# End of each FFN of a streaming encoder step: last down weights split in the scheduled list, the norm's shift taken off in PSUM, last output rows finished on VectorE

## The chip, the cores and the metric

One core of a Trainium2 chip runs the whole program in one launch. The metric is the device time of one execution in microseconds; of several runs the median is taken. Engine names in the profile: PE is TensorE's matmul, PEld its weight load, DVE is VectorE, ACT is ScalarE, POOL is GpSimd, SP is the engine that issues most DMAs.

## What is computed

Two layers of a streaming encoder on 512 prompt rows and 64 sample rows (576 in all) of width 1024, in fp32. Each layer is a mixer and then a gated FFN with a causal convolution of width 3; both are followed by a post-norm. Cut to what matters here:

```python
def layer_norm(x, g, b):
    mu = jnp.mean(x, axis=-1, keepdims=True)
    var = jnp.mean(jnp.square(x - mu), axis=-1, keepdims=True)
    return (x - mu) * lax.rsqrt(var + LN_EPS) * g + b

def conv_ffn(x, conv_state, w_up, conv_w, conv_b, w_down):
    hc, new_state = causal_dwconv(x @ w_up, conv_state, conv_w, conv_b)
    g, u = jnp.split(hc, 2, axis=-1)                 # 2 x 2816 columns
    return (jax.nn.gelu(g) * u) @ w_down, new_state

for layer in range(2):
    xp = layer_norm(ALPHA * xp + mixer(xp), ln_mix_g[layer], ln_mix_b[layer])     # same for xs
    f, new_conv = conv_ffn(xp, state, ffn_w_up[layer], ...)
    xp = layer_norm(ALPHA * xp + f, ln_ffn_g[layer], ln_ffn_b[layer])
```

## The kernel before

The state x lies transposed in SBUF: 8 tiles m of 128 features by 576 rows. Every product is made of three matmuls on numbers split in two: a high part rounded to the matmul's type and the rest as a low part (hh and hl of the hidden state, hi and lo of a weight). The rows go in two halves, so that one product fits a PSUM bank; the halves are 288 and 288 columns, in the last norm (n4) 320 and 256.

A weight comes by DMA into one of four `raw` buffers (SP). ScalarE copies it into the high part and VectorE subtracts that for the low part: a split (lines 307 and 308 outside the list below, 1277 and 1280 in it). `pump` (line 291) makes the next split of the weights in the order of the program, if its load has been issued and a slot is free; a freed buffer lets SP issue the next load.

The middle of an FFN is written as a list, `Plan`. Each operation names its engine, its cost, what it reads and what it writes; matmuls stay in the program's order and give due times, and each other engine takes the ready operation that is due first. An operation that no matmul in the list depends on has no due time and is taken when its engine has nothing else that is ready. The list holds the 22 blocks of the hidden width, each with its up weights, convolution, gelu and product, and the down products, which go through the list in chunks. The last chunk (blocks 17 to 21, 5 k-tiles) has 8 weights `dl[0]` to `dl[7]`, one for each tile m of x, 640 columns wide. The products of m = 0, 1, 2 stand at the end of the list (matmuls of line 1202, six banks, k outermost: 18 matmuls for each k). Block 21's hidden part is written last and is read by their last k. In the list the splits of m = 0 to 4 are made; the slots of m = 4 to 7 are those of the up weights of block 21.

After the list come, in program order on each engine: the posts of m = 0 and 1 (VectorE adds a bank to a tile of x, line 486, and sums tile 0 and tile 1 to `s1r`, line 489); two transposes that bring out the new conv state; then a `sweep` over m = 3 to 7 for the first half of the rows and a `sweep` for the second (matmuls of lines 417 to 419). A hook c of a sweep is called when c triplets of matmuls have gone; a weight has 5 triplets.

- `weights(5)`, `weights(6)`, `weights(7)` at hooks 1, 6 and 8 make the splits of m = 5, 6, 7.
- `shift` at hook 4: the norm takes off a common shift, which keeps its sums small. One matmul for each half turns `s1r` into the mean over the 256 features of tiles 0 and 1, on all partitions (`mone4` holds 4/1024, line 497); ScalarE copies it to `cs`; VectorE subtracts it from all 8 tiles, both halves: 16 instructions (line 507). Tiles 3 to 7 get their last product later, on top of it. Then m = 2 is posted.
- `acc` (lines 522 to 530) follows each tile: ScalarE squares it, the squares are summed to `a2` on VectorE (line 514), and the tiles to `a1`, on GpSimd for the early tiles and VectorE for the last. `a1` takes `s1r`'s buffers.
- Pumps at hooks 13, 17 and 21 (first FFN alone), for the first weights of the next layer.
- In the second sweep: `stats` of the first half (line 545, single-column matmuls on `a1` and `a2`, then small VectorE and GpSimd instructions, line 550 on), and the normalisation.

In the last FFN the second half of the output is different: `fin_early` at hooks 5, 9 and 13 transposes x's tiles 0 to 3 for the row blocks 0 to 2 (line 1758), since the output is by rows. The blocks 0 to 2 are finished within the second sweep (`fin_a`), blocks 3 and 4 at the end: `fin_q0` on VectorE for the left 512 columns (lines 1788, 1790), `fin_norm` on ScalarE for the right ones (line 1795), then `fin_q1`, a multiply and an add, block 4's on VectorE and block 3's on GpSimd (lines 1799, 1800). `fin_out` (line 1771) issues each output on SP, 256 KB.

Memory: the norm's pool `lnp` is opened at the left after the list, in the place of the list's sums of x; the FFN's pool is closed after the conv state's output.

## Time and profile before

| | us |
|---|---|
| median of 3 runs | 1305.2 (1304.25 to 1306.86) |
| profiled execution | 1306.91 |
| its span, first to last instruction | 1304.7 |
| PE busy in the span | 1243.1 |
| DVE busy | 1020.2 |
| ACT busy | 665.4 |
| POOL busy | 603.8 |

The span is what the trace covers; the rest of the execution lies around it. Busy time of an engine is an average over stages. The end of the first FFN lies at about 640 to 690 us, that of the last at about 1240 to 1305.

### The profile page before, as it was taken

Reading aid. Unit: us, or ns where it says so; the run is one execution under the profiler, and the core shown is the slowest. Engines: PE = TensorE matmul, PEld = TensorE weight load, DVE = VectorE, ACT = ScalarE, POOL = GpSimd, SP = SyncE. Lnnn points to the kernel's source line nnn. Section 1 sums busy time; section 2 is a strip of 40 time slices with the busy share of each in tenths; the row PEclk is TensorE's granted clock in tenths of the full one; section 3 lists DMA queues with packets and bytes.
Section 4 is the critical chain, followed back from the end, with each engine's and each line's share of the span. In section 5 each row is a group of like instructions: output and inputs, shape, how many; then the busy total and the mean of one; then the engine's idle time right before and its main releaser. Section 6 shows DMA issues by size and latency. Waiting matters only on the chain.

```text
span 1304.7 us, 23742 instructions
## 1 busy us (share of the span) xinstructions
PE 1243.1 (95%) x9087; PEld 1201.6 (92%) x9087; DVE 1020.2 (78%) x1895; ACT 665.4 (51%) x1064; POOL 603.8 (46%) x652
## 2 busy tenths in 40 slices
PE   8999999998999999999979998998999999999974
PEld 8999888998999999999979788998999999999974
DVE  4547786789998989887775339878999898878767
ACT  4553544457565556565343232347656566556432
POOL 3223222676465457364163015666654656545124
PEclk9999999999999999999979998999999999999987
DMA  8416320307675867666131422214657668866412
GB/s 224 127 33 183 99 82 14 100 12 169 147 168 128 191 150 177 153 159 145 56 97 49 145 65 73 68 35 101 155 140 180 141 147 192 170 150 147 93 36 73
DMA packets 204565, 155.76 MB, mean 119 GB/s; under 512 B 6524, under 2 KB 187036, under 8 KB 204452
## 3 DMA queue, kind: packets, MB, share of 16 engines
q1 hardware_dynamic: 192324, 111.96, 30.1%
q0 software_dynamic: 12128, 42.30, 18.3%
q8 instruction: 71, 1.16, 0.4%
q14 instruction: 42, 0.34, 0.1%
HBM read 107.07 MB, written 5.22 MB: 86 GB/s over the span
## 4 chain that ended last, share of the span: by engine, by line
PE 67%; DVE 14%; issue 9%; ACT 4%; POOL 3%; DMA 2%; ACTq 0%; SPq 0%; DVEq 0%; POOLq 0%
PE mm L1202 32%; PE aux L1202 16%; PE mm L417 4%; PE mm L418 4%; PE mm L419 4%; POOL x L585 2%; DVE x L507 1%; DVE raw L1355 1%; DVE wloA L308 1%; PE aux L545 1%; PE o L1094 1%; DMA wloB<-raw 1%; DVE x L486 1%; DVE pt L1045 1%; ACT pt L1041 1%
## 5 line engine op out<-in xcount | busy, mean ns | idle before, releaser
L1315 DVE SCALAR_TENSOR_TENSOR y<-hb,vecF,y 128x578 f32<-128x578 f32 x176 | 165.8, 970 | 6.3 <-ACT y L1305 4.9
L308 DVE TENSOR_TENSOR wloA<-raw,whiA 128x1024 fp32r<-128x1024 f32 (+2 forms) x54 | 65.3, 1225 | 98.4 <-ACT whiA L307 98.4
L1202 PE MATMUL mm<-xh,wloB 128*128 128x288 f32 x384 | 113.6, 296 | 0.0
L1202 PE MATMUL mm<-xh,whiB 128*128 128x288 f32 x384 | 113.5, 296 | 0.0
L1202 PE MATMUL mm<-xl,whiB 128*128 128x288 f32 x384 | 113.5, 296 | 0.0
L1254 POOL TENSOR_TENSOR raw<-raw 128x512 f32<-128x512 f32 x40 | 59.3, 1482 | 88.2 <-DVE wloB L1252 38.3
L1202 PE MATMUL mm<-xh,whiA 128*128 128x288 f32 x320 | 94.7, 296 | 5.4 <-ACT xh L1370 3.6
L417 PE MATMUL mm<-xh,whiA 128*128 128x288 f32 (+2 forms) x320 | 96.6, 302 | 3.2 <-ACT xh L641 3.2
L419 PE MATMUL mm<-xh,wloA 128*128 128x288 f32 (+2 forms) x320 | 95.2, 298 | 1.5 <-DVE wloA L308 1.5
L1202 PE MATMUL mm<-xl,whiA 128*128 128x288 f32 x320 | 95.2, 297 | 1.0 <-DVE xl L1372 1.0
L418 PE MATMUL mm<-xl,whiA 128*128 128x288 f32 (+2 forms) x320 | 95.3, 298 | 0.5 <-DVE xl L642 0.5
L1202 PE MATMUL mm<-xh,wloA 128*128 128x288 f32 x320 | 94.8, 296 | 0.0
L1329 POOL COPY stage<-hb 128x4 f32<-128x4 f32 x88 | 51.3, 680 | 90.8 <-DVE hb L1474 71.9
L1305 ACT ACTIVATE y<-hb,vecF 128x578 f32<-128x578 f32 x88 | 74.6, 865 | 32.1 <-DVE hb L1474 21.8
L307 ACT ACTIVATE whiA<-raw 128x1024 fp32r<-128x1024 f32 (+2 forms) x54 | 54.5, 1022 | 61.8 <-PE mm L817 44.4
L1438 DVE TENSOR_TENSOR x<-x,aux 128x288 f32<-128x288 f32 x160 | 71.2, 448 | 17.8 <-PE aux L1202 16.8
L1202 PE MATMUL aux<-hh,wloA 128*128 128x288 f32 x272 | 80.4, 295 | 1.5 <-DVE wloA L1413 1.5
L1202 PE MATMUL aux<-hh,whiA 128*128 128x288 f32 x272 | 80.5, 296 | 0.3
L1202 PE MATMUL aux<-hh,whiB 128*128 128x288 f32 x272 | 80.3, 295 | 0.0
L1202 PE MATMUL aux<-hh,wloB 128*128 128x288 f32 x272 | 80.2, 295 | 0.0
L1202 PE MATMUL aux<-hl,whiA 128*128 128x288 f32 x272 | 80.1, 294 | 0.0
L1202 PE MATMUL aux<-hl,whiB 128*128 128x288 f32 x272 | 80.0, 294 | 0.0
(432 smaller groups left out, 4712.0 us busy)
## 6 DMA issues: line engine op xcount, KB each, us to landing
raw<-in_ffn_w_up_dram SPq DMA_DIRECT2D x88, 512.0 KB
wloA<-raw POOLq DMA_DIRECT2D x40, 512.0 KB, 5.1
wloB<-raw POOLq DMA_DIRECT2D x40, 512.0 KB, 4.9
draw<-in_ffn_w_down_dram SPq DMA_DIRECT2D x80, 192.0 KB
raw<-in_w_in_o_dram SPq DMA_DIRECT2D x16, 512.0 KB
raw<-in_w_in_e_dram SPq DMA_DIRECT2D x14, 512.0 KB
raw<-in_ffn_w_down_dram SPq DMA_DIRECT2D x16, 320.0 KB
raw<-in_w_out_e_dram SPq DMA_DIRECT2D x8, 512.0 KB
```

What stands on the lines that cost most here:

```text
L307: ACT.activation(u.hi[:, c], u.raw[:, c], AF.Copy)
L308: DVE.tensor_sub(u.lo[:, c], u.raw[:, c], u.hi[:, c])
L417: PE.matmul(o, wh, h[:, k, a:b], start=first, stop=False)
L418: PE.matmul(o, wh, l[:, k, a:b], start=False, stop=False)
L419: PE.matmul(o, wl, h[:, k, a:b], start=False, stop=last)
L585: POOL.tensor_scalar(xk, xk, g, bb, op0=OP.mult, op1=OP.add)
L1202: PE.matmul(bank[key][:, :w], lhs(), rhs(), start=first, stop=stop)
L1254: plan.add("POOL", 1.3, lambda: POOL.tensor_add(R(2, b_), R(2, a_), R(2, b_)), r2, r2[1:], True, tag=f"s1_{j}")
L1305: plan.add("ACT", 0.86, lambda: ACT.activation(y, t[:, 2:580], AF.Identity, scale=V[:, 88 + ct:89 + ct], bias=V[:, 132 + ct:133 + ct]), hr ...
L1315: plan.add("DVE", 0.82, lambda q=q, y=y, t=t, ct=ct: DVE.scalar_tensor_tensor(y, t[:, q:q + 578], V[:, 44 * q + ct:44 * q + ct + 1], y, op ...
L1329: plan.add("POOL", 0.4, lambda s=s, t=t: POOL.tensor_copy(stage[:, :, s * NJ + j].rearrange("p (a b) -> p a b", a=2), t[:, 448:580].rearra ...
L1438: DVE.tensor_add(xm, xm, bank[key][:, :H2])
```

## The change

- `split_plain` is called for all 8 last down weights, so that m = 5, 6 and 7 are split in the list, too; the hooks `weights` are gone.
- In a norm that follows an FFN (`short`), `shift` subtracts from tiles 0 and 1 alone. For every other tile and half one more matmul, with `nmone4` = -4/1024, goes into the bank that holds the tile's last product (`unshift`, through `extra` in `sweep`), so that the post adds the shifted value. `a1` gets buffers of its own, since `s1r` is read until the last bank.
- `shift` stands at hook 2 instead of 4, the pumps of the first FFN at 5, 9 and 13 instead of 13, 17 and 21, `fin_early` at 12, 17 and 22 instead of 5, 9 and 13.
- The conv state's output goes ahead of the posts of m = 0 and 1, and the FFN's pool is closed before the norm's is opened.
- Blocks 3 and 4: the right 512 columns are read out of PSUM by VectorE with the mean taken off and the gain multiplied, and scaled with the bias added in a second instruction; ScalarE and GpSimd have no part in it, and each of the four outputs follows its own instruction.

```diff
--- before.py
+++ after.py
@@ -358,6 +358,8 @@
     DVE.memset(ones, 1.0)
     mone4 = consts.tile([128, 8], FR, name="mone4")
     DVE.tensor_scalar(mone4, mone, 4.0, None, op0=OP.mult)
+    nmone4 = consts.tile([128, 8], FR, name="nmone4")
+    DVE.tensor_scalar(nmone4, mone, -4.0, None, op0=OP.mult)
     nhalf = consts.tile([128, 8], FT, name="nhalf")
     DVE.memset(nhalf, -0.5)
     cmask = ev.tile([128, 128], FT, name="cmask")
@@ -418,7 +420,7 @@
         PE.matmul(o, wh, l[:, k, a:b], start=False, stop=False)
         PE.matmul(o, wl, h[:, k, a:b], start=False, stop=last)
 
-    def sweep(us, half, h, l, post, outer=False, hooks=None, ks=None):
+    def sweep(us, half, h, l, post, outer=False, hooks=None, ks=None, extra=None):
         hooks = dict(hooks or {})
         cnt = 0
         ks = ks or list(range(us[0].nk))
@@ -429,9 +431,11 @@
                 hooks.pop(c)()
             if banks[i] is None:
                 banks[i] = mmbank()
-            triplet(banks[i], us[i], k, h, l, half, k == ks[0], k == ks[-1])
+            triplet(banks[i], us[i], k, h, l, half, k == ks[0], k == ks[-1] and extra is None)
             cnt += 1
             if k == ks[-1]:
+                if extra is not None:
+                    extra(half, banks[i])
                 post(i, half, banks[i])
         for c in sorted(hooks):
             hooks[c]()
@@ -497,7 +501,7 @@
                 PE.matmul(bk[:, :b - a], mone4[:, 0:1].to_broadcast([128, 128]), self.s1r[half], start=True, stop=True)
                 self.cs[half] = self.tmp("cs", half)
                 ACT.activation(self.cs[half], bk[:, :b - a], AF.Copy)
-            for m in (2, 3, 0, 1, 4, 5, 6, 7):
+            for m in (0, 1) if self.short else (2, 3, 0, 1, 4, 5, 6, 7):
                 for half in range(2):
                     a, b = self.halves[half]
                     xm = x[:, m, a:b]
@@ -507,6 +511,11 @@
                         (DVE if m < 6 or self.short else POOL).tensor_sub(xm, xm, self.cs[half])
                     if m < 2:
                         self.acc(m, half)
+
+        def unshift(self, half, bk):
+
+            a, b = self.halves[half]
+            PE.matmul(bk[:, :b - a], nmone4[:, 0:1].to_broadcast([128, 128]), self.s1r[half], start=False, stop=True)
 
         def drain(self, half):
             if half in self.pend:
@@ -524,7 +533,7 @@
             sq = lnp["p"].tile([128, self.W], FT, name="sq", bufs=3)[:, :b - a]
             ACT.activation(sq, xm, AF.Square)
             if m == 1:
-                self.a1[half] = self.tmp("s1r", half)
+                self.a1[half] = self.tmp("a1" if self.short else "s1r", half)
                 POOL.tensor_add(self.a1[half], x[:, 0, a:b], xm)
             else:
                 (DVE if m >= self.dve else POOL).tensor_add(self.a1[half], self.a1[half], xm)
@@ -1552,7 +1561,7 @@
         for j in range(2, NJ):
             window(up[j], up.get(j + 1), j - 1, DOWNS[j])
         assert dn["run"] == len(dq)
-        for m in range(5):
+        for m in range(8):
             split_plain(dl[m], m // 4, m % 4)
         tail_of(NJ - 1)
         cut["h"] = norm.halves
@@ -1563,25 +1572,14 @@
                     s = dl[0].slots[k]
                     w = sl(0, m)
                     for n, (e, q) in enumerate(((0, 0), (0, 1), (1, 0))):
-                        mm(("K", m, half), kb[m, half], k == 0 and n == 0, k == dl[0].nk - 1 and n == 2,
+                        mm(("K", m, half), kb[m, half], k == 0 and n == 0, k == dl[0].nk - 1 and n == 2 and m < 2,
                            lambda m=m, e=e, k=k: (dl[m].hi, dl[m].lo)[e][:, 128 * k:128 * k + 128],
                            lambda q=q, s=s, a=a, b=b: (hh, hl)[q][:, s, a:b], (w[2 * e + k // 4], ("hidden", s, "hl"[q])), w=b - a,
                            took=0.0065 + (b - a) * 0.000439, tag=f"K{m}.{half}")
         plan.emit()
         st["dma"], st["freed"] = loaded["dma"], loaded["freed"]
         tes.close()
-        open_ln()
         banks = {k: bank["K", k[0], k[1]] for k in kb}
-        for i in range(2):
-            for half in range(2):
-                norm.post(i, half, banks[i, half])
-        live["A"] -= 3
-
-        def plain_split(u, w):
-            u.hi, u.lo = w
-            split_part(u, 0)
-            free_raw(1)
-
         bk = auxbank()
         sT = ytile()[:88, :256].rearrange("p (q c) -> p q c", q=2)
         for q in range(2):
@@ -1592,26 +1590,31 @@
             nc.sync.dma_start(dram(O[12 + q], layer * 4 * DFF, [[128, 88], [1, 128]]), sT[:, q])
         fes.close()
 
+        open_ln()
+        for i in range(2):
+            for half in range(2):
+                norm.post(i, half, banks[i, half])
+        live["A"] -= 3
+
         def shift():
             norm.shift()
             for half in range(2):
+                norm.unshift(half, banks[2, half])
                 norm.post(2, half, banks[2, half])
 
-        def weights(m):
-            return lambda: plain_split(dl[m], S[1][m - 4])
-
-        return dl[3:8], {1: weights(5), 4: shift, 6: weights(6), 8: weights(7)}
+        return dl[3:8], {2: shift}
 
     def ffn_tail(rest, norm):
         us, hooks = rest
-        hooks.update({c: pump for c in (13, 17, 21)})
+        hooks.update({c: pump for c in (5, 9, 13)})
         post = lambda i, hf, b: norm.post(3 + i, hf, b)
-        sweep(us, 0, hh, hl, post, hooks=hooks)
+        sweep(us, 0, hh, hl, post, hooks=hooks, extra=norm.unshift)
         hooks = norm.hooks(0, (7, 9, 11, 15))
-        sweep(us[0:1], 1, hh, hl, post)
+        sweep(us[0:1], 1, hh, hl, post, extra=norm.unshift)
         live["A"] -= 1
         pump(1)
-        sweep(us[1:], 1, hh, hl, lambda i, hf, b: post(i + 1, hf, b), hooks={c - 5: f for c, f in hooks.items()})
+        sweep(us[1:], 1, hh, hl, lambda i, hf, b: post(i + 1, hf, b), hooks={c - 5: f for c, f in hooks.items()},
+              extra=norm.unshift)
 
     n2 = Norm(("ln_ffn_g", 0), ("ln_ffn_b", 0), False, short=True)
     ffn_tail(ffn(0, n1, n2), n2)
@@ -1811,10 +1814,10 @@
         fin_shift(0)
 
     post = lambda i, hf, b: n4.post(3 + i, hf, b)
-    hooks = {5 + 4 * q: (lambda q=q: fin_early(q)) for q in range(3)}
+    hooks = {12 + 5 * q: (lambda q=q: fin_early(q)) for q in range(3)}
     hooks.update(last_hooks)
-    sweep(dl, 0, hh, hl, post, hooks=hooks)
-    sweep(dl, 1, hh, hl, post,
+    sweep(dl, 0, hh, hl, post, hooks=hooks, extra=n4.unshift)
+    sweep(dl, 1, hh, hl, post, extra=n4.unshift,
           hooks={4: stats_a, 6: lambda: fin_early(3), 8: lambda: fin_a(0), 11: lambda: fin_early(4),
                  13: lambda: fin_a(1), 18: lambda: fin_a(2)})
     qb = {}
@@ -1825,14 +1828,17 @@
         fin_t(blk, 1, qb[blk], 3, 4)
     n4.stats(1)
     fin_shift(1)
-    fin_q0(3, False)
-    fin_q0(4, False)
     for blk in (3, 4):
-        fin_norm(blk, qb[blk][:FB[blk][1]])
-    fin_q0(3, True)
-    fin_q0(4, True)
-    fin_q1(4, DVE, DVE)
-    fin_q1(3, POOL, POOL)
+        fin_q0(blk, False)
+    for blk in (3, 4):
+        _, y1, mu, rs, nm, n = fin_parts(blk)
+        DVE.scalar_tensor_tensor(y1, qb[blk][:n], mu, gB2[:n, 512:], op0=OP.subtract, op1=OP.mult)
+    for blk in (3, 4):
+        fin_q0(blk, True)
+    for blk in (3, 4):
+        _, y1, mu, rs, nm, n = fin_parts(blk)
+        DVE.scalar_tensor_tensor(y1, y1, rs, bB2[:n, 512:], op0=OP.mult, op1=OP.add)
+        fin_out(blk, 1)
     fes.close()
     wes["es"].close()
     close_ln()
```

## Rows read from the trace of the kernel before

**Rows 1.** The page: busy time, share of the span and instructions of each engine.

```profile
PE 1243.1 (95%) x9087; PEld 1201.6 (92%) x9087; DVE 1020.2 (78%) x1895; ACT 665.4 (51%) x1064; POOL 603.8 (46%) x652
```

**Rows 2.** Stretches: length, busy (instructions) PE, PEld, DVE, ACT, POOL, PEclk, DMA share, GB/s.

```profile
650.00:655.00 5.00, 1.39 (x11) 1.15 (x9) 5.00 (x14) 1.54 (x5) 4.79 (x3) 1.00 0.08 25
...
1250.00:1255.00 5.00, 1.47 (x7) 0.75 (x6) 4.55 (x13) 2.23 (x6) 1.50 (x1) 0.82 0.69 219
1255.00:1260.00 5.00, 1.46 (x5) 1.17 (x6) 4.63 (x11) 1.78 (x4) 5.00 (x4) 0.50 0.01 2
```

**Rows 3.** Timeline, PE, end of first FFN: start, length, instruction [idle before <-releaser].

```profile
645.83 0.29 PE L417 MATMUL mm<-hh,whiA 128*128 128x288 f32 x1
...
646.62 0.42 PE L497 MATMUL aux<-s1r,mone 128*128 128x288 f32 x2
...
656.90 0.61 PE L417 MATMUL mm<-hh,whiB 128*128 128x288 f32 x1 [5.51 <-ACT whiB L307]
...
669.53 1.12 PE L545 MATMUL aux<-mone,s1r 128*96 128x1 f32 x6 [2.84 <-DVE s1r L530]
...
688.25 0.64 PE L545 MATMUL aux<-mone,s1r 128*96 128x1 f32 x6 [1.40 <-DVE s1r L530]
```

**Rows 4.** Timeline, DVE, the same stretch.

```profile
647.39 5.99 DVE L507 TENSOR_TENSOR x<-x,cs 128x288 f32<-128x288 f32 x16 [0.24 <-ACT cs L499]
653.30 0.45 DVE L486 TENSOR_TENSOR x<-x,mm 128x288 f32<-128x288 f32 x1
653.66 0.69 DVE L514 TENSOR_TENSOR a<-a,sq 128x288 f32<-128x288 f32 x1
654.27 0.44 DVE L486 TENSOR_TENSOR x<-x,mm 128x288 f32<-128x288 f32 x1
...
660.93 1.22 DVE L308 TENSOR_TENSOR wloA<-raw,whiA 128x1024 fp32r<-128x1024 f32 x1 [1.15 <-ACT whiA L307]
...
669.02 0.45 DVE L530 TENSOR_TENSOR s1r<-s1r,x 128x288 f32<-128x288 f32 x1
...
672.86 0.15 DVE L550 COPY sb<-aux 96x6 f32<-96x6 f32 x1
```

**Rows 5.** Timeline, PE, end of the last FFN.

```profile
1245.46 0.31 PE L1202 MATMUL mm<-hh,whiA 128*128 128x320 f32 x1
...
1248.95 0.31 PE L417 MATMUL mm<-hh,whiA 128*128 128x320 f32 x1
...
1259.02 0.47 PE L1758 MATMUL aux<-ident,x 128*128 128x128 f32 x1 [1.46 <-DVE x L486]
...
1265.13 0.60 PE L1758 MATMUL aux<-ident,x 128*64 128x128 f32 x4
1265.48 0.39 PE L417 MATMUL mm<-hh,whiB 128*128 128x320 f32 x1
...
1270.84 0.28 PE L417 MATMUL mm<-hh,whiA 128*128 128x256 f32 x1
```

**Rows 6.** Timeline, DVE, the same stretch.

```profile
1242.63 0.76 DVE L1325 TENSOR_TENSOR hl<-y,hh 128x576 fp32r<-128x576 f32 x1 [0.75 <-ACT hh L1324]
...
1248.27 0.42 DVE L489 TENSOR_TENSOR s1r<-x 128x256 fp32r<-128x256 f32 x1
1249.37 0.83 DVE L308 TENSOR_TENSOR wloB<-raw,whiB 128x640 fp32r<-128x640 f32 x1 [0.67 <-ACT whiB L307]
1250.64 5.99 DVE L507 TENSOR_TENSOR x<-x,cs 128x320 f32<-128x320 f32 x16 [0.45 <-ACT cs L499]
```

**Rows 7.** Timeline, DVE, the last output rows.

```profile
1292.72 1.41 DVE L1788 SCALAR_TENSOR_TENSOR raw<-raw,sb,gB 128x512 f32<-128x512 f32 x2
...
1297.23 1.63 DVE L1800 TENSOR_TENSOR raw<-raw,bB 128x512 f32<-128x512 f32 x1
```

**Rows 8.** Timeline, SP (the DMA queue's issues), the end.

```profile
1298.89 0.81 SPq L1771 DMA_DIRECT2D out_dram<-raw  x2
```

**Rows 9.** Stretches, columns as in Rows 2, the last outputs' data.

```profile
1300.00:1301.00 1.00, 0.00 (x0) 0.00 (x0) 0.00 (x0) 0.00 (x0) 0.00 (x0) 0.50 1.01 377
```

## The prediction

> **What bounds the kernel now.** I read the page's busy shares first: TensorE is busy 95% of the span [rows 1]. So the change can only win where TensorE stands or runs at half clock. The table by stretches shows two such places, the ends of the two FFNs [rows 2]: in 650 to 655 and in 1250 to 1260 us TensorE is busy 1.4 to 1.5 us of each 5 while VectorE is busy 4.5 to 5.0, and in 1255 to 1260 the granted clock is 0.50, the lower of its two levels. The lists by engine tell why. In the first FFN TensorE waits 5.51 us for the split of a down weight (ScalarE) and later 2.84 us for the sums of the norm (VectorE) [rows 3]. ScalarE and VectorE work in order, and that split is queued behind the norm's shift: 16 subtractions in one run of 5.99 us [rows 4]. In the last FFN the same run of 16 [rows 6] holds up the early transposes of x; the last of them to wait, at 1259.02, ends the gap [rows 5].
>
> **The sum by parts.** The profiled execution took 1306.91 us, its span 1304.7, so 2.2 us lie around the span; it is 1.7 us above the median of the three runs. I work out what is saved in it and take that off both.
>
> *Splits into the scheduled list.* Three splits per FFN (m = 5, 6, 7) move ahead of the last products. One costs 0.83 us on VectorE behind a wait of 0.67 for its ScalarE half [rows 6]. Their slots come free one after the other while the last pair's products run, so they meet block 21 on its way through both engines. Its last write ends at 1243.39 (1242.63 + 0.76) [rows 6]; the first matmul of the last k, which reads it, starts at 1245.46 [rows 5]. So there are 2.07 us of cover. One or two of the VectorE halves can slip into short waits of that chain, and push it by less than 0.83 each; I take nothing. If all three splits went ahead of it with both halves, 3 x (0.83 + 0.67) = 4.5 less 2.07 would be 2.4 us per FFN. The freed raw buffers also queue more loads on SP, in the first FFN of the next layer's weights; behind them on SP is only the conv state's output, for which no compute waits.
>
> *Shift in PSUM.* Only tiles 0 and 1 are still subtracted on VectorE, 4 instructions of 16. The 16 took 5.91 us, from 647.39 to the next instruction at 653.30 [rows 4], 0.37 each, so 12 x 0.37 = 4.4 us leave VectorE per FFN. TensorE gets 12 more matmuls per FFN, of 288 columns like the six between 645.83 and 646.62 [rows 3], 0.13 each: 1.6 us. They count, since TensorE then sets the pace. That a weight is loaded for one matmul each is nothing new: every matmul here has its own. The shift comes two triplets earlier; in the last FFN the s1r that it reads is done at 1248.69 (1248.27 + 0.42) [rows 6], before TensorE gets there at 1248.95 [rows 5], so that wait is nothing, at most 0.1.
>
> *First FFN.* The shift moves from 646.62 to 645.83 [rows 3], 0.79, so the subtractions start at 646.6 and end at 648.1. Tile 2, two halves: an add of 0.36 and a running sum of 0.61 (653.30, 653.66, 654.27) [rows 4] each, 650.0; tile 3, 651.0. Now the pumps stand here: three splits of 1.22 us, each behind a wait of 1.15 for ScalarE [rows 4]. The first waits about 1.0, two then run together at some 1.4 each (1.22, and up to 1.6 by the ratio of 0.61 to 0.36, since GpSimd adds meanwhile): 654.8. Tile 4, add and sum at 0.37 each, 655.5; the third split with its wait 657.8; tiles 5 to 7 at 0.73 and what the last sum waits for GpSimd's, 660.05. In the kernel before, that last sum starts at 669.02 [rows 4]: 9.0 us. TensorE itself would be at the statistics at 645.83 + (4 + 90 + 6) x 0.133 = 659.1 (shift, matmuls, shifts of single banks) and would wait 1.3 there in place of the two waits of 5.51 and 2.84. What follows, to the copy of the statistics at 672.86 [rows 4] and on to the second statistics at 688.25, where TensorE waited 1.40 for VectorE [rows 3], is VectorE's queue in the same order, so the 9.0 stay. Ends: the work that leaves the queue ahead of the last sum, 4.4 + 3 x 0.83 = 6.9; TensorE's own arrival, 669.53 - 659.1 = 10.4. I take 9.0, since the waits in it are counted.
>
> *Last FFN.* TensorE from 1248.95: 4 shift matmuls 0.53; 69 matmuls of 320 columns at 0.147 (0.133 x 320/288) 10.1; 5 single shifts 0.74; three groups of transposes at 0.35 (1265.13 to 1265.48) and a slow matmul behind each [rows 5], 1.3: 1261.7. Before, the second half starts at 1270.84 [rows 5]: 9.2 us. Condition: the first transposes, now at 1254.2, find x ready. VectorE: subtractions from 1249.7 (0.77 behind the shift's matmul, as 647.39 behind 646.62), four of them 1251.2, tile 2 twice 1253.2, tile 3's add 1253.6. That is 0.6 us to spare, so no wait. Ends: 8.0, if they wait 0.6 and half clock for some matmuls follows; 9.2. The second half is VectorE's, whose queue holds GpSimd-slowed work up to 1290; it is unchanged and moves as a whole, and its 5 extra matmuls (0.6 us) lie in TensorE's slack.
>
> *Last rows.* Before: two scalings on ScalarE, then a multiply and an add per block, one block on VectorE and the other on GpSimd, which slow each other (1.63 us for one instruction on VectorE [rows 7], 0.70 without). VectorE ends at 1298.86, and the last two outputs leave only then, at 1298.89 [rows 8]. After: from 1292.72 eight VectorE instructions at 0.70 (two took 1.41) [rows 7], 5.6, end 1298.3: 0.5 earlier; and one output of 256 KB stands behind the end instead of two, 0.7 us at 377 GB/s [rows 9]. Sum 1.2. Ends: 0.5, if the outputs queue up anyway, and 1.3. The trace has no such instruction with a first operand in PSUM; the nearest rows are an add of 288 columns from PSUM at 0.45 and one from SBUF at 0.45 [rows 4], so I take no difference; by their spread it is 0.05 either way.
>
> The Trainium skill, "ScalarE: Activation LUTs", section "Step-by-step: what each stage is for", places ScalarE closer to PSUM and VectorE closer to SBUF, which speaks against moving these reads to VectorE. The two adds do not show it, 0.45 against 0.45. If it cost a tenth of each of the two reads, an estimate, the last part would be 1.1.
>
> Sum: 9.0 + 9.2 + 1.2 = 19.4. For a run like the profiled one 1306.91 - 19.4 = 1287.5; for the median 1305.2 - 19.4 = 1285.8.
>
> **The rivals.**
> B, VectorE's queue eats part of it: the pumps now stand ahead of tile 4, among GpSimd's sums, and only the removed work is saved. For it: sums of 0.61 beside GpSimd's, where the subtractions go at 0.37 [rows 4]. Against: the pumps stood in the same queue before. 6.9 + 8.0 + 0.5 = 15.4: 1289.8.
> C, the splits delay block 21: 2.4 us per FFN, and if the clock then falls, the last 18 matmuls cost double, 2.5 more; twice 4.9, 1295.6. For it: nothing in the list is due after them, so no due time orders them. Against: one at a time they fit into waits.
> D, the norm's pool is opened after the FFN's is closed, and its first tile could lie where the state's output is still read; the first s1r would wait for that transfer. Price by the time from the outputs' issue at 1298.89 [rows 8] to the end of their data at about 1301 [rows 9]: some 2.2 us, with the clock's fall as much again, 4.4, twice: 1294.6. Against: by the sizes of the tiles, the pool reaches only with its last bytes into the old place, and those hold the statistics.
> E, slower: a split in the list stands at the head of ScalarE's queue for a raw load that has not landed, and block 21's gelu behind it. It costs what the load is late beyond 2.07 us and decides from 2.07 + 9.7 = 11.8 us per FFN; at 14 us, 1309.7. For it: the load of m = 7 can only be issued when the split of m = 3 has freed its buffer. Against: in the kernel before these loads are issued at the same point of the list, and its list of VectorE shows no wait for one.
>
> **How the numbers follow.** Forecast 0.62 (1282.5 to 1288, its ends and a run spread of 1.3), B 0.17 (1288 to 1292), C 0.10, D 0.06, E 0.03, no change 0.02. 1282 to 1292 leaves out C, D, E and tails, about 2 in 10. Faster by over 0.2% (2.6 us, about what a measurement of this kernel can tell from no change) 0.95, same 0.02, slower 0.03.
>
> **What would show it.** Right: TensorE busy nearly 5 of 5 us at full clock in the 10 us behind both last products; runs of 4 subtractions instead of 16; no wait of 5.5 us for a split; the first statistics 9 us earlier; the last outputs leaving one by one. Wrong: a gap ahead of the last k (C, E), s1r late (D), a wait at the transposes at 1254 (the 0.6 us were not there), or a wait for the statistics far over 1.3 us in the first FFN (B).

## The result, and the profile after

The changed kernel takes 1285.38 us (median of four, 1283.31 to 1287.51), the kernel before, beside it on the same chip, 1305.65 us. The ratio is 0.984, with a 95% interval of 0.9825 to 0.9854: 20.3 us less, where 19.4 were forecast. The profiled execution took 1287.51 us, its span 1285.5, which is the slowest of the four; so 19.2 us lie between the two spans.

To say where they come from I cut each span at VectorE's instructions that stand in every version: the first add of a bank to x behind an FFN's list, the copy of the norm's first statistics, that of its second statistics, and the end. For the kernel before the two copies of the first FFN are at 672.86 [rows 4] and 689.44 us, those of the last one at 1274.04 and 1292.18. In us:

| kernel | to the first FFN's list end | its list end to 1st statistics | 1st to 2nd | to the last FFN's list end | its list end to 1st statistics | 1st to 2nd | 2nd to the end |
|---|---|---|---|---|---|---|---|
| before | 643.02 | 29.84 | 16.57 | 556.66 | 27.94 | 18.14 | 12.52 |
| after | 643.71 | 21.36 | 16.66 | 557.79 | 18.74 | 18.19 | 9.07 |
| difference | +0.69 | -8.48 | +0.09 | +1.13 | -9.20 | +0.05 | -3.45 |

The two long stretches, in which the change is not or nearly not at work, move by a us or two from one execution to the next: over the ten kernels profiled here the first is 641.7 to 643.7 and the other 554.9 to 559.5. The short ones repeat to 0.1 or 0.2 us wherever their code is the same. So they can be compared from kernel to kernel, and the rest of this document does that.

The page's busy times, to set beside [rows 1]: TensorE 1238.7 us (4.4 less), VectorE 1010.2 (10 less), GpSimd 592.6 (11 less).

The stretches of the kernel after behind the two lists (columns as in [rows 2]). TensorE is busy all the time at full clock where it was busy 1.4 to 1.5 of 5 us before; what is left of the hole in the first FFN stands in 660 to 665, around the statistics.

```profile
650.00:655.00 5.00, 5.00 (x40) 5.00 (x39) 4.10 (x6) 2.79 (x4) 3.26 (x4) 1.00 0.00 0
655.00:660.00 5.00, 4.96 (x38) 4.72 (x36) 3.85 (x8) 2.06 (x4) 1.79 (x2) 1.00 0.66 222
660.00:665.00 5.00, 2.68 (x18) 2.36 (x18) 3.81 (x8) 2.10 (x4) 1.84 (x2) 0.79 0.29 94
...
1245.00:1250.00 5.00, 5.00 (x37) 4.99 (x36) 4.22 (x10) 2.50 (x6) 4.49 (x5) 1.00 0.55 156
1250.00:1255.00 5.00, 5.00 (x38) 4.96 (x37) 2.51 (x7) 2.14 (x4) 0.00 (x0) 1.00 0.00 0
```

The timeline of TensorE in the kernel after, first FFN (start, length, instruction, idle time before it and its releaser). L501 is the shift's matmul of [rows 3], L518 the new one that takes the shift off in the bank. No matmul of this stretch waits for a split any more; the first that waits is the statistics'.

```profile
646.51 0.43 PE L501 MATMUL aux<-s1r,mone 128*128 128x288 f32 x2
646.77 0.43 PE L518 MATMUL mm<-s1r,nmone 128*128 128x288 f32 x2
...
661.78 1.15 PE L554 MATMUL aux<-mone,a 128*96 128x1 f32 x12 [1.83 <-DVE a L539]
```

VectorE's timeline in the same stretch, from block 21 on. To be read beside [rows 4]: the subtractions (L511) are four and not 16, the splits of the last weights (L1289) stand ahead of block 21's last write (L1334), and the pumps (L308) ahead of the sums of the late tiles. L539 at 661.19 is the last sum, at 669.02 before; L559 is the copy of the statistics.

```profile
631.04 1.55 DVE L1289 TENSOR_TENSOR wloB<-raw,whiB 128x640 fp32r<-128x640 f32 x2
...
640.73 0.76 DVE L1334 TENSOR_TENSOR hl<-y,hh 128x576 fp32r<-128x576 f32 x1 [0.75 <-ACT hh L1333]
643.71 1.24 DVE L490 TENSOR_TENSOR x<-x,mm 128x288 f32<-128x288 f32 x3 [2.22 <-PE mm L1211]
...
647.29 1.56 DVE L511 TENSOR_TENSOR x<-x,cs 128x288 f32<-128x288 f32 x4 [0.98 <-ACT cs L503]
...
652.72 2.76 DVE L308 TENSOR_TENSOR wloA<-raw,whiA 128x1024 fp32r<-128x1024 f32 x2 [0.90 <-ACT whiA L307]
...
657.36 1.22 DVE L308 TENSOR_TENSOR wloA<-raw,whiA 128x1024 fp32r<-128x1024 f32 x1 [1.15 <-ACT whiA L307]
...
659.60 0.70 DVE L523 TENSOR_TENSOR a<-a,sq 128x288 f32<-128x288 f32 x1
660.23 0.44 DVE L490 TENSOR_TENSOR x<-x,mm 128x288 f32<-128x288 f32 x1
660.59 0.68 DVE L523 TENSOR_TENSOR a<-a,sq 128x288 f32<-128x288 f32 x1
661.19 0.45 DVE L539 TENSOR_TENSOR a<-a,x 128x288 f32<-128x288 f32 x1
...
663.93 1.22 DVE L308 TENSOR_TENSOR wloA<-raw,whiA 128x1024 fp32r<-128x1024 f32 x1 [1.19 <-ACT whiA L307]
665.07 0.15 DVE L559 COPY sb<-aux 96x6 f32<-96x6 f32 x1
```

And GpSimd's adds beside the two sums of 0.70 and 0.68:

```profile
659.09 1.86 POOL L539 TENSOR_TENSOR a<-a,x 128x288 f32<-128x288 f32 x2 [2.22 <-DVE x L490]
```

The last FFN of the kernel after, TensorE and then VectorE. The three groups of early transposes (L1761, at 1247.59, 1250.38 and 1253.16) start without a wait. The first group reads tile 3's first half, whose add starts at 1246.64 and ends at 1247.11, 0.48 us ahead of 1247.59.

```profile
1247.59 0.60 PE L1761 MATMUL aux<-ident,x 128*128 128x128 f32 x4
```
```profile
1246.64 0.47 DVE L490 TENSOR_TENSOR x<-x,mm 128x320 f32<-128x320 f32 x1
```

The last rows of the kernel after, VectorE: eight instructions, in four pairs (the third, at 1279.64, is left out below). Each pair takes 1.40 or 1.41 us, with the first operand in SBUF (L1791) or in PSUM (L1835).

```profile
1277.00 1.41 DVE L1791 SCALAR_TENSOR_TENSOR raw<-raw,sb,gB 128x512 f32<-128x512 f32 x2
1278.32 1.40 DVE L1835 SCALAR_TENSOR_TENSOR raw<-mm,sb,gB 128x512 f32<-128x512 f32 x2
...
1280.97 1.41 DVE L1840 SCALAR_TENSOR_TENSOR raw<-raw,sb,bB 128x512 f32<-128x512 f32 x2
```

And the end of both programs: GpSimd's last instruction before (block 3's add, span 1304.7) and the stretch in which the last data move; then the same of after (span 1285.5). Behind these stretches nothing moves.

```profile
1296.73 1.59 POOL L1800 TENSOR_TENSOR raw<-raw,bB 128x512 f32<-128x512 f32 x1
```
```profile
1301.00:1302.00 1.00, 0.00 (x0) 0.00 (x0) 0.00 (x0) 0.00 (x0) 0.00 (x0) 0.50 0.12 43
```
```profile
1278.40 0.20 POOL L1786 TENSOR_TENSOR sb<-sb 128x2 f32<-128x2 f32 x1
```
```profile
1283.00:1284.00 1.00, 0.00 (x0) 0.00 (x0) 0.00 (x0) 0.00 (x0) 0.00 (x0) 0.50 0.98 377
```

Before, the data have all moved at about 1301.1, and the program ends 3.6 us later; after, at 1284.0, and it ends 1.5 us later. That is the part of the result that the prediction has no step for, and the first experiments are about it.

What fills this time stands in the rows of the line that encloses the whole program (`with _tile.TileContext(nc) as tc:`), which is closed at the program's end (a small q behind the engine's name means its queue; the three numbers are the shortest, the middle and the longest duration in ns, then come the first and the last start). Before, then after:

```profile
L1868 POOLq EVENT_SEMAPHORE  x4: 17/17/17, 1304.0 to 1304.6; - x4
L1868 POOLq DRAIN  x3: 46/93/7228, 1296.7 to 1304.4; - x3
L1868 SPq DRAIN  x3: 7/7/7, 1301.9 to 1304.2; - x3
```
```profile
L1874 POOLq DRAIN  x3: 46/97/5835, 1278.4 to 1285.2; - x3
L1874 SPq DRAIN  x3: 7/7/7, 1284.7 to 1285.0; - x3
```

The longest of GpSimd's three DRAINs is the first; the other two stand in the last 0.6 us. It ends at 1303.9 before (1296.7 + 7.23) and at 1284.2 after (1278.4 + 5.84). In both kernels that is 5.6 us behind the end of GpSimd's last instruction (1298.32 and 1278.60). Before, the exchange of semaphores that closes the program begins right behind it, at 1304.0, though SP's queue, which waits for the outputs, has been through since 1301.9. After, GpSimd's drain is over 0.5 us ahead of SP's, and the outputs decide.

### The profile page after: what moved, and what is told of

It reads as the page before. It is cut to its first block, busy times and chain, and to the rows that moved or that the text cites. A ratio compares the mean times of both kernels' runs of the same rounds, so it can differ in the third digit from the quotient of the medians.

```text
span 1285.5 us, 23770 instructions
## 1 busy us (share of the span) xinstructions
PE 1238.7 (96%) x9111; PEld 1198.7 (93%) x9111; DVE 1010.2 (79%) x1874; ACT 664.6 (52%) x1062; POOL 592.6 (46%) x650
## 4 chain that ended last, share of the span: by engine, by line
PE 70%; DVE 13%; issue 9%; ACT 3%; POOL 3%; DMA 2%; DVEq 0%; SPq 0%; POOLq 0%; ACTq 0%
PE mm L1211 33%; PE aux L1211 17%; PE mm L419 4%; PE mm L420 4%; PE mm L421 4%; POOL x L594 2%; DMA wloB<-raw 1%; DVE raw L1364 1%; DVE wloA L308 1%; PE o L1103 1%; PE aux L554 1%; DVE vo L1679 1%; DMA raw<-in_w_in_e_dram 1%; ACT whiA L307 1%; PE mm L772 1%
## 5 line engine op out<-in xcount | busy, mean ns | idle before, releaser
L308 DVE TENSOR_TENSOR wloA<-raw,whiA 128x1024 fp32r<-128x1024 f32 (+2 forms) x54 | 65.6, 1232 | 97.3 <-ACT whiA L307 97.3
```

Source lines behind the costliest of these rows:

```text
L308: DVE.tensor_sub(u.lo[:, c], u.raw[:, c], u.hi[:, c])
```

## The experiments

Eight kernels were run, each beside the kernel before on the same chip. All their stretches, in us, as in the table above (without the two long ones):

| kernel | time, median | ratio to before, 95% | first FFN | 1st to 2nd | last FFN | 1st to 2nd | to the end |
|---|---|---|---|---|---|---|---|
| last rows alone | 1301.89 | 0.996 to 0.9986 | 29.84 | 16.49 | 28.05 | 18.13 | 9.11 |
| after, GpSimd touched late | 1288.24 | 0.9841 to 0.9879 | 21.35 | 16.74 | 18.75 | 18.19 | 12.61 |
| after, old last rows | 1287.30 | 0.9842 to 0.9874 | 21.34 | 16.61 | 18.74 | 18.20 | 12.52 |
| splits alone | 1303.97 | 0.9975 to 0.9994 | 27.64 | 16.60 | 28.21 | 18.14 | 12.52 |
| matmul on the bank alone | 1296.73 | 0.9907 to 0.9959 | 25.47 | 16.55 | 22.14 | 18.31 | 12.52 |
| after, old hooks | 1291.24 | 0.9858 to 0.9901 | 23.27 | 16.56 | 23.69 | 18.20 | 9.07 |
| after, three edits more | 1282.55 | 0.9803 to 0.9832 | 18.27 | 19.04 | 18.75 | 15.36 | 9.07 |
| after, two of the three | 1281.55 | 0.9792 to 0.982 | 20.38 | 17.31 | 18.75 | 15.37 | 9.06 |

### The last rows alone

The kernel before with the change's last rows and nothing else of it.

```diff
-    fin_q0(3, False)
-    fin_q0(4, False)
     for blk in (3, 4):
-        fin_norm(blk, qb[blk][:FB[blk][1]])
-    fin_q0(3, True)
-    fin_q0(4, True)
-    fin_q1(4, DVE, DVE)
-    fin_q1(3, POOL, POOL)
+        fin_q0(blk, False)
+    for blk in (3, 4):
+        _, y1, mu, rs, nm, n = fin_parts(blk)
+        DVE.scalar_tensor_tensor(y1, qb[blk][:n], mu, gB2[:n, 512:], op0=OP.subtract, op1=OP.mult)
...
```

> The kernel before with only the last rows' finish of the changed kernel (blocks 3 and 4 finished on VectorE alone). Theory 1, formed from the two traces: when GpSimd works on the last rows, its own finishing at the end of the program (5.6 us from its last instruction at 1298.32 to its part of the final exchange of semaphores at 1303.96) ends later than the last output's landing (1301.60); without it the program ends 3.5 us earlier than the kernel before, and the time from the last copy of statistics to the end of the span falls from 12.5 to about 9.0 us. Theory 2, the prediction: 0.5 us from VectorE's end and 0.7 from one output less in the queue, 1.2 us in all, 12.5 to 11.3 us.

Measured: the end is 9.11 us behind the last statistics, where it was 12.52: 3.41 less. The rest stays, and the time falls by 4.3 us (1306.23 to 1301.89). So the last rows bring nearly three times the 1.2 us of the prediction, by themselves.

### GpSimd touched late

The changed kernel with one copy of two columns on GpSimd behind VectorE's last instruction. It is written to a place that nobody reads afterwards.

```diff
         fin_out(blk, 1)
+    POOL.tensor_copy(n4.st[1][:, 12:14], yts[4][:, 1022:1024])
```

> The changed kernel with one GpSimd copy of 128x2 numbers behind the last VectorE instruction of the last rows; the outputs are the same. Theory 1 (GpSimd's finishing): its last instruction now ends at about 1282.6 on the changed kernel's clock, so the span ends some 5.6 to 6.2 us later, at about 1288.5: 3 us longer than the changed kernel, 1288 us in time, the time from the last copy of statistics to the end 12 us instead of 9.0. Theory 2 (the outputs set the end): no more than 0.2 us.

GpSimd's last instruction in this kernel (span 1285.1), the stretch in which the last data move, and GpSimd's drains:

```profile
1278.51 0.18 POOL L1842 COPY sb<-raw 128x2 f32<-128x2 f32 x1 [3.91 <-DVE raw L1840]
```
```profile
1279.00:1280.00 1.00, 0.00 (x0) 0.00 (x0) 0.00 (x0) 0.00 (x0) 0.00 (x0) 0.50 0.98 377
```
```profile
L1875 POOLq DRAIN  x3: 46/98/5797, 1278.5 to 1284.8; - x3
```

Measured: 12.61 in place of 9.07, 3.5 us for an instruction of 0.18 us that no output waits for. The data have moved at 1280.0, as early behind the statistics (7.5 us) as in the changed kernel, and the program ends 5.1 us later instead of 1.5. From GpSimd's last instruction to the end it is 1285.1 - 1278.69 = 6.4 us; in the kernel before 1304.7 - 1298.32 = 6.4 as well. 5.6 us of that are the drain, which ends at 1284.3 (1278.5 + 5.80); SP's queue has been through since 1280.7. What GpSimd does within the drain no row shows.

### The changed kernel with the old last rows

```diff
+    fin_q0(3, False)
+    fin_q0(4, False)
     for blk in (3, 4):
-        fin_q0(blk, False)
...
+        fin_norm(blk, qb[blk][:FB[blk][1]])
+    fin_q0(3, True)
+    fin_q0(4, True)
+    fin_q1(4, DVE, DVE)
+    fin_q1(3, POOL, POOL)
```

> The changed kernel with the last rows put back as the kernel before had them (ScalarE out of PSUM, and GpSimd's two operations of the fourth block at the end); all else stays. Theory (the program's end is the later of two ends: the last output's landing, and GpSimd's last operation with some 5.6 us of finishing behind it): the stretch behind the last statistics is 12.5 us again instead of 9.07, and the whole 3.4 us longer, about 1288.8. Rival (the prediction's own term: only the last landing counts): 1.2 to 1.4 us longer, about 1286.7.

GpSimd's last instruction in it (span 1284.6):

```profile
1276.61 1.59 POOL L1803 TENSOR_TENSOR raw<-raw,bB 128x512 f32<-128x512 f32 x1
```

Measured: 12.52 behind the statistics, 3.45 more than 9.07, to the hundredth as in the kernel before; and from GpSimd's end at 1278.20 it is 6.4 us again. The whole was 1.9 us longer, not 3.4; the profiled execution has its other gains in the two long stretches (642.16 and 555.00), which move by that much by themselves. The stretch decides for the theory, the whole alone would not.

### The splits alone

The kernel before with all eight splits in the list.

```diff
-        for m in range(5):
+        for m in range(8):
...
-        return dl[3:8], {1: weights(5), 4: shift, 6: weights(6), 8: weights(7)}
+        return dl[3:8], {4: shift}
```

> The kernel before with only the splits of m = 5, 6 and 7 moved into the list. Theory of the prediction, by parts: the three splits (0.83 and 2.17 us with GpSimd beside them, and waits of 0.71 and 0.60 for ScalarE) leave VectorE's queue ahead of the first statistics in the first FFN, about 4.3 us there; in the last FFN the gap ends with tile 3's post, which no split delays, so 0 to 0.3 us. In all 4 to 4.6 us faster than before, and the wait of 5.51 us for a split is gone. Rival: the split's wait was the whole loss in the first FFN, 5.5 us and the half clock behind it 2.5: 8 us faster. Rival C: block 21 is delayed beyond its 2.07 us of cover, and it is less than 4.

TensorE's wait in the first FFN, and the last of its waits in the last one:

```profile
666.06 1.09 PE L545 MATMUL aux<-mone,s1r 128*96 128x1 f32 x6 [8.56 <-DVE s1r L530]
```
```profile
1255.14 0.48 PE L1758 MATMUL aux<-ident,x 128*128 128x128 f32 x1 [1.46 <-DVE x L486]
```

Measured: 2.2 us in the first FFN, of the 4.3 expected, and nothing in the last one (0.27 more). The wait of 5.51 us for a split [rows 3] is gone, and the one for the sums has grown from 2.84 to 8.56. With the split out of its way TensorE only comes earlier to what VectorE has not done. What VectorE gained shows in its list. In the kernel before, two of the three splits stand together in it; in this kernel a pump comes next. Before, then this kernel, with its run of 16 subtractions:

```profile
656.88 2.17 DVE L308 TENSOR_TENSOR wloB<-raw,whiB 128x640 fp32r<-128x640 f32 x2 [0.60 <-ACT whiB L307]
```
```profile
646.07 5.99 DVE L507 TENSOR_TENSOR x<-x,cs 128x288 f32<-128x288 f32 x16 [1.77 <-ACT cs L499]
...
656.88 1.73 DVE L308 TENSOR_TENSOR wloA<-raw,whiA 128x1024 fp32r<-128x1024 f32 x1 [0.90 <-ACT whiA L307]
```

The first of the three splits had cost nothing: it stood where VectorE otherwise waits for `cs`, and the subtractions start 4.37 us behind the first add in both kernels (647.39 - 643.02 and 646.07 - 641.70). The other two held VectorE 2.69 us with their wait (from 656.28 to the next instruction at 658.97). Of that 0.5 is lost again: the sum and the pump that come next now run beside GpSimd's adds, the pump in 1.73 us instead of 1.22. That leaves the 2.2, and the expected 4.3 had counted the first split and its wait, too.

### The matmul on the bank alone

The kernel before with the shift of tiles 2 to 7 taken off in PSUM, with the splits, hooks and last rows of before. The conv state's output stands ahead of the posts, as in the changed kernel.

```diff
-            for m in (2, 3, 0, 1, 4, 5, 6, 7):
+            for m in (0, 1) if self.short else (2, 3, 0, 1, 4, 5, 6, 7):
...
+                if extra is not None:
+                    extra(half, banks[i])
...
```

> The changed kernel with the splits of m = 5 to 7 back in the hooks, all hooks and the last rows as in the kernel before: what is left is the shift taken off in PSUM (12 subtractions less, 12 matmuls more per FFN) and the order of the conv state's output. Theory: 4.4 us per FFN leave VectorE's queue ahead of what TensorE waits for: first FFN 4.4, last FFN 4.4 to 5.5 (a shorter gap, and less half clock), 9 to 10 us faster than before. Rival: the 12 matmuls at 0.13 and their weight loads eat it, or the gap only shrinks to another wait: below 6 us.

Measured: 4.37 in the first FFN, as expected (4.4), and 5.80 in the last one, a little above the 4.4 to 5.5. It is the largest single part. The conv state's output has no part in it: the subtractions start as long behind the first add as before (4.38 us beside 4.37 in the first FFN, 4.55 beside 4.54 in the last one). TensorE still waits 4.61 us for the sums in the first FFN, and in the last one 2.4 us at the transposes, which are as early as before.

```profile
665.24 2.08 PE L554 MATMUL aux<-mone,a 128*96 128x1 f32 x12 [4.61 <-DVE a L539]
```

### The changed kernel with the old hooks

```diff
-        return dl[3:8], {2: shift}
+        return dl[3:8], {4: shift}
...
-        hooks.update({c: pump for c in (5, 9, 13)})
+        hooks.update({c: pump for c in (13, 17, 21)})
...
-    hooks = {12 + 5 * q: (lambda q=q: fin_early(q)) for q in range(3)}
+    hooks = {5 + 4 * q: (lambda q=q: fin_early(q)) for q in range(3)}
```

> The changed kernel with the hooks of both last sweeps put back to where the kernel before had them: norm's shift in front of triplet 4 instead of 2, the three pumps of the first FFN at 13, 17 and 21 instead of 5, 9 and 13, and the three early transposes of the last FFN at 5, 9 and 13 instead of 12, 17 and 22. Splits in the list, the matmul on the bank and the new last rows stay. Theory (what the splits alone and the matmul alone leave of the change's gain is the hooks'): the first FFN up to its first statistics, 21.4 us in the changed kernel, takes 1.9 us more (8.5 - 2.2 - 4.4), and the last one, 18.7, takes 3.7 us more (9.2 + 0.3 - 5.8), with TensorE standing at the early transposes for tiles 0 to 3 again; all in all 1289 to 1291 beside 1285.4. Rival: the order of the hooks is free, since the matmul on the bank has taken the shift off the path; both stages stay within 0.3 us, and what the two single parts left over is a run-to-run matter: 1285.

TensorE at the first group of early transposes of the last FFN in this kernel, up to the next matmul, and the stretch behind it:

```profile
1244.38 0.33 PE L1761 MATMUL aux<-ident,x 128*128 128x128 f32 x1
1245.12 0.33 PE L1761 MATMUL aux<-ident,x 128*128 128x128 f32 x1 [0.41 <-DVE x L511]
1245.85 0.33 PE L1761 MATMUL aux<-ident,x 128*128 128x128 f32 x1 [0.41 <-DVE x L490]
1247.79 0.33 PE L1761 MATMUL aux<-ident,x 128*128 128x128 f32 x1 [1.61 <-DVE x L490]
1247.87 0.39 PE L419 MATMUL mm<-hh,whiB 128*128 128x320 f32 x1
```
```profile
1249.00:1254.00 5.00, 5.00 (x29) 4.93 (x27) 1.29 (x3) 1.07 (x2) 0.82 (x2) 0.66 0.00 0
```

Measured: 1.91 us more in the first FFN, as expected, and 4.95 in the last one, above the 3.7 that subtraction gave. So the order of the hooks is no small matter: in the last FFN it is worth more than half of the 9.20 (the transposes' places and the shift's together; they were not tried apart). From its first transpose to the next matmul the group takes 3.5 us (1244.38 to 1247.87), in the kernel after 0.35 (1247.59 to 1247.94). Of these 3.1 us more, 2.4 are waits; in the rest the four transposes, 0.33 us each, stand one behind the other, where in the kernel after they overlap. Behind them the granted clock is 0.66 in five us (0.50, the lower of its two levels, from 1249.8 to 1251.8), at which 5 us of matmuls do the work of 3.3 at full clock, 1.7 more. That makes 4.8 of the 4.95.

### Three edits more, and two of them

Three waits of VectorE are left in the kernel after, and three ways to shorten them were tried on it: (a) the three pumps together at one hook, so that VectorE meets ScalarE's copy once, (b) the fourth pump, which stands just ahead of the copy of the statistics (663.93 above, with a wait of 1.19), moved behind the centring, (c) the right 512 columns of blocks 0 to 2 finished on VectorE as the last rows are, without ScalarE and GpSimd. The second kernel has (a) and (c) alone. In this order in the diff:

```diff
-        hooks.update({c: pump for c in (5, 9, 13)})
+        hooks.update({5: lambda: pump(3)})
...
-        pump(1)
-        sweep(us[1:], 1, hh, hl, lambda i, hf, b: post(i + 1, hf, b), hooks={c - 5: f for c, f in hooks.items()},
+        sweep(us[1:], 1, hh, hl, lambda i, hf, b: post(i + 1, hf, b), hooks={**{c - 5: f for c, f in hooks.items()}, 5: pump},
...
-        fin_norm(blk, fin_t(blk, 1, auxbank()))
+        bk = fin_t(blk, 1, auxbank())
+        _, y1, mu, rs, nm, n = fin_parts(blk)
+        DVE.scalar_tensor_tensor(y1, bk, mu, gB2[:n, 512:], op0=OP.subtract, op1=OP.mult)
         fin_q0(blk, True)
-        fin_q1(blk, POOL, POOL)
+        DVE.scalar_tensor_tensor(y1, y1, rs, bB2[:n, 512:], op0=OP.mult, op1=OP.add)
+        fin_out(blk, 1)
```

> The changed kernel with three edits more. (a) First FFN: its three pumped splits run together in front of triplet 5 instead of one each at 5, 9 and 13, so that VectorE meets ScalarE's copy once and not three times. (b) First FFN: the fourth pumped split moves from behind the first unit of the second half, where it stands ahead of the copy of the statistics, to triplet 5 of the rest, between the centring and the scaling. (c) Last FFN: the second 512 columns of the blocks 0 to 2 are finished as the last rows are, by two operations of VectorE out of PSUM, without ScalarE and GpSimd. Theory: (a) saves about 1.2 us and (b) 0 to 1.2 up to the first FFN's first statistics (21.4); (c) leaves VectorE 6 operations at about 0.7 us each in place of operations that are slowed to 1.2 to 1.8 us beside GpSimd's, and saves 2 to 3 us of the 18.2 between the last FFN's two statistics. In all 1280 to 1283. Rival: TensorE sets these stretches (its matmuls are due anyway); (a), (b) and (c) then move VectorE's idle time alone and the time stays at 1285.

> The changed kernel with (a) and (c) of the kernel with three edits, without (b): three pumped splits in front of triplet 5, the fourth stays behind the first unit of the second half, and the blocks 0 to 2 of the last rows on VectorE alone. With the three edits the first FFN took 18.27 + 19.04 us up to its first and its second statistics, 37.3 in all beside 38.0. Theory (the fourth split costs the same on either side of the copy of the first statistics, because it stands in VectorE's row at both places): the first FFN is 37.3 again within 0.2 us, with about 1.2 us more ahead of the copy and 1.2 less behind it, and the last one is as with the three edits; 1282.5. Rival (at triplet 5 the split stands ahead of the scaling, which the next stage waits for, and (b) has cost what (a) saved): the first FFN takes 36.6 to 36.9, and the whole 0.4 to 0.7 us less.

VectorE in the kernel with all three: the three pumps together and the fourth one at its new place, behind the copy of the statistics at 661.65; then block 1 of the last rows, four instructions, of which the third is left out.

```profile
652.39 3.88 DVE L308 TENSOR_TENSOR wloA<-raw,whiA 128x1024 fp32r<-128x1024 f32 x3 [0.91 <-ACT whiA L307]
...
667.04 1.23 DVE L308 TENSOR_TENSOR wloA<-raw,whiA 128x1024 fp32r<-128x1024 f32 x1 [1.09 <-ACT whiA L307]
```
```profile
1261.33 0.75 DVE L1790 SCALAR_TENSOR_TENSOR yt<-yt,sb,gB 128x512 f32<-128x512 f32 x1
1261.99 0.74 DVE L1809 SCALAR_TENSOR_TENSOR yt<-aux,sb,gB 128x512 f32<-128x512 f32 x1
...
1263.32 0.75 DVE L1811 SCALAR_TENSOR_TENSOR yt<-yt,sb,bB 128x512 f32<-128x512 f32 x1
```

In the kernel after, the same block has two instructions of VectorE in place of four, beside GpSimd's:

```profile
1264.77 1.77 DVE L1791 SCALAR_TENSOR_TENSOR yt<-yt,sb,gB 128x512 f32<-128x512 f32 x1
1266.57 1.67 DVE L1793 SCALAR_TENSOR_TENSOR yt<-yt,sb,bB 128x512 f32<-128x512 f32 x1
```

Measured: (c) takes 2.8 us from the stretch between the last FFN's two statistics, 18.19 to 15.36, with twice the instructions on VectorE: four at 0.74 us take 3.0, two beside GpSimd took 3.4. Of (a) and (b) little is left. All three edits take 3.09 us from the stretch up to the first statistics and give 2.38 back behind it, 0.7 in all; (a) without (b) takes 0.98 and gives 0.65 back, 0.3 in all. So without (b) there are 2.1 us more ahead of the copy and 1.7 less behind it, where the theory had 1.2 and 1.2: (b) is worth 0.4 by the stretches. The first FFN takes 37.7 us in all, so the theory's 37.3 within 0.2 is missed, and the rival, that (b) costs what (a) saves (36.6 to 36.9), is farther off still. What gives (a)'s gain back is at least in part GpSimd: without (b), the sum behind the centring takes 1.47 us beside GpSimd's work, where it takes 0.48 in the kernel after.

```profile
666.84 1.47 DVE L523 TENSOR_TENSOR a<-a,sq 128x288 f32<-128x288 f32 x1
```

By their whole times the two kernels can't be told apart (1281.46 to 1283.61 and 1281.17 to 1285.19). Both are below the kernel after (0.9818 and 0.9806 of before, where after is 0.984), by about 3 and 4 us; the interval of the first (0.9803 to 0.9832) still overlaps that of the kernel after.

## Why the prediction came out

**The time.** The sum of 19.4 stands beside 20.3 in the medians. By stretches it is 8.5 for 9.0, 9.2 for 9.2 and 3.45 for 1.2, so the terms sum to 21.1, 1.7 above the forecast; the medians fall 0.8 short of that, no more than the long stretches move. So it is partly luck that the total came within 0.9 us: the last rows brought 2.3 more than their term, and 0.5 less in the first FFN and the 0.8 hide more than half of that.

**Last FFN, 9.2: right, with its condition.** TensorE runs through with no wait for VectorE up to the first statistics, and the transposes find x ready with 0.48 us to spare, where the step had 0.6. That the condition counts is shown by the experiment: with the hooks at their old places, the transposes seven to nine triplets earlier and the shift two later, the stretch is 4.95 us longer.

**First FFN, 9.0: right but for its last 0.5.** The path can be checked from point to point, after taking off the 0.69 us by which the list ended later. The subtractions start at 646.60 (forecast 646.6); behind the third pump the next instruction starts at 657.81 (658.50 - 0.69; forecast 657.8); TensorE is at the statistics at 659.26 (661.78 - 1.83 - 0.69; forecast 659.1). The last sum starts at 660.50, forecast 660.05. The 0.45 between are the two sums at 659.60 and 660.59: they hold VectorE 0.63 and 0.60 us, up to the next instruction's start at 660.23 and 661.19, where I had 0.37 each. GpSimd's two adds run beside them, from 659.09 to 660.95. I had priced that slowing for the sums of tile 2 and for the pumps, and not for the last ones. The add between them, at 660.23, reads one operand in PSUM and is not slowed, 0.44 us. This agrees with the Trainium skill, "SBUF — State Buffer", section "Who interferes with whom", by which an instruction of VectorE with two operands in SBUF contends with one of GpSimd that reads SBUF, and one with at most one operand there, outside VectorE's two-port modes, does not. So TensorE waits 1.83 and not 1.3.

**Last rows, 1.2: the term that was mis-sized.** Its own two parts are there. VectorE ends 5.92 us behind the last statistics in place of 6.68, 0.76 for 0.5, and the last data have moved at 7.5 us in place of 8.9 behind the statistics, 1.4 for 1.2. The step that failed is the one taken without a word, that the program ends when the last output has landed. It ended 3.6 us after the data before and ends 1.5 us after them now. In the five kernels where GpSimd works late (an add of 512 columns in four of them, a copy of two columns in the fifth) the end stands 6.4 us behind GpSimd's last instruction, while it stands 3.6 us behind the last data in the four and 5.1 in the fifth. In the five where GpSimd has no part in the last outputs, the end is 1.5 us behind the data. In all ten the drain of GpSimd's queue ends 5.6 us behind GpSimd's last instruction, and the closing exchange begins when both this drain and SP's wait for the outputs are over. The end is the later of the two. In the changed kernel GpSimd's comes 0.5 us ahead of the outputs', so outputs that land still earlier could gain no more than that. The row stood in the trace of before: a DRAIN of 7.23 us on GpSimd's queue.

**The splits, nothing.** The term was right: TensorE is busy 5.00 of 5 us at full clock in all of 630 to 645 and waits for nothing there (C, E). The splits do slip in ahead of block 21, two at 631.04, and block 21's last write ends 0.4 us later, counted from its place in the list; VectorE's wait behind it is still 2.22 us. That the splits by themselves bring so little, 2.2 and -0.3 us, fits the sum: VectorE's queue set the pace, and its work had to be cut before TensorE could use the time.

**The rivals.** B (15.4 us in all) falls with the stretches. D falls with VectorE's list: the sums to `s1r` follow at once (the first at 644.99). E's wait for a raw load does not occur. That VectorE reads from PSUM as cheaply as from SBUF is now measured: two instructions of 512 columns take 1.40 us with the first operand in PSUM and 1.41 in SBUF. What the Trainium skill, "ScalarE: Activation LUTs", section "Step-by-step: what each stage is for", says of the two engines' places is not seen in these rows.

## What to carry to other kernels

When two in-order engines hold each other up, find the one whose queue is full and take work out of that one; removing the wait that the profile names on the other can do little but lengthen its next wait, as here 5.51 and 2.84 us became one of 8.56. An instruction moved a few places in the program, so that its input is ready when the engine gets there, can be worth as much as the work removed. And look at what lies between the last data and the end of the span: if it is more in one kernel than in another, look in the rows of the line that encloses the program for the queue whose drain ends last, and give its engine nothing late to do. Here it was GpSimd's.

## What the runs showed of the hardware

GpSimd's last instruction had 6.4 us behind it before the program could end, whether it was long or short: 5.6 us up to the end of a DRAIN on its queue, the same in all ten kernels, and 0.8 of closing exchange. A copy of two columns, 0.18 us long, behind the last work cost 3.5 us. I had not expected this; what GpSimd does within the drain is not shown.

Two instructions of VectorE beside GpSimd's elementwise work took 1.77 and 1.67 us, and 0.74 each without it. Where both engines share a job of this kind, giving all of it to VectorE was faster by 2.8 us over three blocks.
